# Where the sums of weights are copied and when their users wait: a two-layer Mamba-2 / attention trunk in split fp32 on one core

## The chip, the cores and the metric

One NeuronCore of a Trainium2 chip runs the whole program. The metric is the device time of one execution in microseconds. TensorE multiplies, VectorE (DVE) and ScalarE (ACT) work on tiles, GpSimd (POOL) does a few small operations and issues some DMAs, SyncE (SP) issues most DMAs.

## What is computed

The input has 256 tokens of 2048 features, in float32. Two layers work on it; each is a mixer with a residual and a SwiGLU with a residual. The first mixer is Mamba-2 (input projection, convolution, scan, gate, output projection); after layer 0 shared keys, values and forget gates are made, and the second mixer is attention with a forget bias. The part that the change touches is the SwiGLU:

```python
def swiglu(h, w_gate_up, w_down):      # h: 256 x 2048, w_gate_up: 2048 x 11264, w_down: 5632 x 2048
    g, u = jnp.split(h @ w_gate_up, 2, axis=-1)
    return (jax.nn.silu(g) * u) @ w_down
```

All weights, some 460 MB, are read from DRAM once.

## The kernel before

**Split products.** Each float32 operand is split into a rounded part `hi` and a rest `lo`; a product is three matmuls, `x_hi w_hi`, `x_hi w_lo` and `x_lo w_hi` (L562 to L564 in plain blocks, L475 to L478 in crossed groups). A load brings 128 x 1024 weights (two tiles of k by 512 columns, 512 KB) into one of six buffers `wraw`; ScalarE casts it to `whi` (L270), VectorE subtracts to get `wlo` (L276), four pieces ahead of TensorE (`SPL`).

**Blocks and pairs.** A block is 512 columns of output for all 256 tokens, in two PSUM banks `acc`. The sum over k goes in groups `kg` of 512 rows. In the output, up and down projections two neighbouring blocks make a pair (`pair`, L335): the left and the right block. In the up projection they are 512 columns of gate and the same 512 of up; 11 pairs stand in each layer. Some of the groups of a pair are "crossed": instead of eight products of (half of k) x (half of the tokens) x (block), seven products of sums do, as in Strassen's scheme (42 matmuls in place of 48). The seven are called a to g. Their products go to the two blocks' own banks (g and b to the left, f to the right) and to four more PSUM banks of the pool `mis` (d, c, a, e). The sums of activations are made on the chip (`sums_of`, L610, with a ScalarE pass over the transposes in PSUM; `add_sums`, L631, afterwards from the split halves). Of the sums of weights, in the up projection two (`c` and `a`) are made in DRAM ahead of time ("made"), and two more on VectorE between the splits (L429).

**Sums in DRAM.** A `Sum` is a DRAM tile of 512 KB: a copy of one piece of the weights, to which another is then added by an accumulating DMA. `next_sum` (L368) issues the copies of this sum and of the one after it (L377) and this sum's accumulate (L378), all in GpSimd's queue; the accumulate waits until its copy has landed. `stream` calls it before each eighth load (`PACE`, L511); were a sum still missing when its load is issued, `load` would make it there (L392). There are 84, 42 a layer.

**Order of the up projection.** With `made` and groups 1 and 2 crossed (pairs 0 to 9), a pair goes: left of group 0, right of group 0, group 1 (order "fdcaegb"), left of group 3, group 2, right of group 3. The last pair crosses group 2 alone. With the product d of a pair's first group the program issues all that is pending in the urgent and the middle list (L463), such as the transposes and splits of the blocks of `h` that the stage before has just finished. Those, too, use the banks of `mis`.

**Evictions.** With the product e, `took` (L768) starts `parts` (L732): `d` is copied out of PSUM, then VectorE makes `v = e - d`, `y = c - v`, `v = a + v`, `u = v - c`. When the left block is done, `gate` (L743) adds its two banks to `d` and `y` (which frees them for the next pair's left block) and ScalarE takes SiLU of them; when the right block is done, `up` (L751) adds its banks to `v` and `u`, multiplies, transposes and splits the result.

**Start of an up projection.** `out_stage` (L697) ends each mixer: it adds the blocks to `h`, transposes and splits them into the next stage's slots (`take`, L712), with sums of activations for the groups named in `summed` (1 and 2), sums of squares, and at the end the rsqrt of the norm on GpSimd (L581).

**Queues.** Each engine takes its instructions in the order in which the program issued them. SyncE issues the loads, each waiting until its `wraw` buffer is free. GpSimd's queue holds the copies and accumulates of the sums, the rsqrts and a few loads of the scan.

Of the kernel before, what the change touches and what calls it, by code (L numbers as in the profile page):

```python
# [9 lines left out]
F32 = mybir.dt.float32  # L10
F32R = mybir.dt.float32r
AF = mybir.ActivationFunctionType
ALU = mybir.AluOpType
# [4 lines left out]
P = 128  # L18
# [4 lines left out]
NB = 512  # L23
# [6 lines left out]
NFB = DFF // NB  # L30
# [6 lines left out]
WOUT, DN0, DN1 = (4, 6), (3, 7), (3, 6, 9)  # L37
# [1 line left out]
WARM = 9  # L39
RAW = 6  # L40
SPL = 4
PACE = 8


LAT = 0.4
# [4 lines left out]
C_AN, C_F0, C_KV, C_BN, C_F1 = 0, 16, 32, 48, 64  # L50
# [179 lines left out]
def kernel(ctx: ExitStack, tc: tile.TileContext, xT_d, x_d, cols_d, rows_d, wdt_d, win_d,  # L230
# [17 lines left out]
    def nm(s):  # L248
        uid[0] += 1
        return f"{s}_{uid[0]}"  # L250
# [114 lines left out]
            order.append(both[0].after)  # L365
        blocks.append(order + rights)

    def next_sum(n=1):  # L368

        for _ in range(n):  # L370
            i = next((i for i, v in enumerate(sums) if not v.made), None)
            if i is None:
                return
            for v in sums[i:i + 2]:
                if v.tile is None:
                    v.tile = dram.tile([P, 2, NB], F32, name=nm("wsum"))
                    nc.gpsimd.dma_start(out=v.tile, in_=v.one)  # L377
            nc.gpsimd.dma_start(out=sums[i].tile, in_=sums[i].other, accum_op=ALU.add)  # L378
            sums[i].made = True

    def slot_of(s):
        t = None
# [108 lines left out]
    def stream(pre_load, pre_split):  # L491
        pieces, units = [], []
        for b in blocks:
            for u in b.units if isinstance(b, Block) else b:
                if isinstance(u, Group):
                    pieces += [(u, n) for n in u.cross.order]
                    units += u.units.values()
                else:
                    pieces += [(u, ks) for ks in u.pieces]
                    units.append(u)  # L500
        parts = {}
        loaded, dead = [0], [0]

        def load_on():
            while dead[0] < len(units) and units[dead[0]].dead:
                dead[0] += 1
            while loaded[0] < min(dead[0] + RAW, len(units)):
                i = loaded[0]
                if i in pre_load:
                    pre_load[i]()  # L510
                if i % PACE == PACE - 1:  # L511
                    next_sum()
                load(units[i], i == 0, load_x0 if i < 2 else None)
                loaded[0] += 1

        def split_to(n):
            for i in range(len(parts), min(n, len(pieces))):
                u, js = pieces[i]
                if i in pre_split:
                    pre_split[i]()  # L520
                parts[i] = split_cross(u, js) if isinstance(u, Group) else split_piece(u, js)
                load_on()

        load_on()
        split_to(SPL - 1)
        held = deque()
        for i, (u, ks) in enumerate(pieces):
            split_to(i + SPL)
            if isinstance(u, Group):
                cross_step(u, ks, parts[i])  # L530
                continue
            b = u.blk
            nk = KT * len(b.xs)
            hi, lo, ready = parts[i]
            flow.work("E", 0.0, ready)
            if u.width < NB:
                if b.ps is None:
                    b.ps = bank([2 * u.width, T])
                for j, k in enumerate(u.ks[n] for n in ks):
                    both = hi[:, j].rearrange("p a n -> p (a n)")  # L540
                    s = slot_of(b.xs[k // KT])
                    nc.tensor.matmul(b.ps, lhsT=both, rhs=s[:, 0, k % KT, :], start=k == 0, stop=False)
                    nc.tensor.matmul(b.ps, lhsT=both, rhs=s[:, 1, k % KT, :], start=False, stop=k == nk - 1)
                flow.work("E", 0.22 * len(ks))
                if ks is u.pieces[-1]:
                    b.task = spawn(b.done(b.ps))
                continue
            if b.ps is None:
                held.append(b)
                if len(held) > 2:  # L550
                    flow.finish(held.popleft().task, evac=True)
                b.ps = [acc.tile([P, u.width], F32, tag="acc", name=nm("acc")) for _ in range(NT)]
            last = b.after is None and u is b.units[-1] and ks is u.pieces[-1]
            order = [(j, t) for j in range(len(ks)) for t in range(NT)]
            if last:
                order = [(j, t) for t in range(NT) for j in range(len(ks))]
            for n, (j, t) in enumerate(order):
                k = u.kg * KT + u.ks[ks[j]]
                s = slot_of(b.xs[k // KT])
                xh = s[:, 0, k % KT, t * P:(t + 1) * P]  # L560
                xl = s[:, 1, k % KT, t * P:(t + 1) * P]
                nc.tensor.matmul(b.ps[t], lhsT=xh, rhs=hi[:, j, :], start=u is b.units[0] and ks[j] == 0, stop=False)  # L562
                nc.tensor.matmul(b.ps[t], lhsT=xh, rhs=lo[:, j, :], start=False, stop=False)  # L563
                nc.tensor.matmul(b.ps[t], lhsT=xl, rhs=hi[:, j, :], start=False,  # L564
                                 stop=last and j == len(ks) - 1)
                if n % 2 == 1:
                    flow.work("E", STEP)
                    flow.pump()
            if last:
                finish_block(b)  # L570
        flow.finish_all()
# [4 lines left out]
    def rsqrt_of(ss, n, width):  # L576

        ms = tiny(width, "ms")
        nc.vector.tensor_scalar(out=ms, in0=ss, scalar1=1.0 / n, scalar2=EPS, op0=ALU.mult, op1=ALU.add)  # L579
        r = tiny(width, "rs")  # L580
        nc.gpsimd.tensor_tensor(out=r, in0=ms, in1=mhalf[:, :width], op=ALU.pow)  # L581
        return r
# [93 lines left out]
    def tt(out, in0, in1, op=ALU.add):  # L676
        nc.vector.tensor_tensor(out=out, in0=in0, in1=in1, op=op)  # L677
        return V(0.66)
# [15 lines left out]
            yield tt(r1, r1, w)  # L694
        return run

    def out_stage(xs, w_d, wcol, crossed, summed=()):  # L697

        ss = const.tile([P, NT, 4], F32, name=nm("ss"))
        nxt = [Slot(j in summed) for j in range(4)]  # L700
        r = [None]

        def done(j):
            def run(ps):
                for t in range(NT):
                    hb = h[:, t, j * NB:(j + 1) * NB]
                    yield tt(hb, hb, ps[t])
                yield EVAC
                nxt[j].task = spawn(take(j), flow.mid)
            return run  # L710

        def take(j):  # L712
            yield SYNC
            yield from h_slot(nxt[j], j, wcol)
            for t in range(NT):
                sumsq(h[:, t, j * NB:(j + 1) * NB], ss[:, t, j:j + 1])
                yield A(0.6)
            if j == 3:
                tot = tiny(NT, "tot")
                nc.vector.tensor_reduce(out=tot, in_=ss, axis=AX.X, op=ALU.add)  # L720
                r[0] = rsqrt_of(tot, DM, NT)

        for j in (0, 2):
            pair(xs, w_d[j:j + 2], (done(j), done(j + 1)), nxt[j:j + 2], crossed, parts_to_h(j))
        return nxt, r

    def ffn_up(xs, r, gu_d, summed):
# [4 lines left out]
        def parts(x):  # L732
            m = x.ps
            d, v, y, u = (tok(i) for i in ("d", "v", "y", "u"))
            x.part = d, y, v, u
            nc.scalar.copy(out=d, in_=m["d"])
            yield A(0.48)
            yield tt(v, m["e"], d, sub)
            yield tt(y, m["c"], v, sub)
            yield tt(v, m["a"], v)  # L740
            yield tt(u, v, m["c"], sub)

        def gate(x, ps):  # L743
            for t, g in enumerate(x.part[:2]):
                yield tt(g, ps[t], g)
            yield EVAC
            for t, g in enumerate(x.part[:2]):
                nc.scalar.activation(g, g, AF.Silu, scale=r[0][:, t:t + 1])
                yield A(0.6, SILU)
# [15 lines left out]
        for nb in range(NFB):  # L765
            x = [None]

            def took(y, x=x):  # L768
                x[0] = y
                return parts(y)  # L770

            pair(xs, gu_d[2 * nb:2 * nb + 2], (lambda ps, x=x: gate(x[0], ps), lambda ps, x=x, nb=nb: up(x[0], ps, nb)),
                 (None, acts[nb]), (1, 2) if nb < NFB - 1 else (2,), took, made=True)
        return acts


# [306 lines left out]
    for g in range(G):  # L1083
        wide(xs1, win_d[12 + g], z_done(g))

    xs2, r2 = out_stage(ys, wout_d, C_F0, WOUT, summed=(1, 2))
    act0 = ffn_up(xs2, r2, gu0_d, DN0)


# [176 lines left out]
        else:  # L1266
            wide(xsq, wv_d[j], v_done(j), wcol=C_KV)

    xs4, r4 = out_stage(oT, wo_d, C_F1, (2,), summed=(1, 2))
    act1 = ffn_up(xs4, r4, gu1_d, DN1)  # L1270
    out_v = out_d.rearrange("(t p) d -> p t d", p=P)

# [107 lines left out]
```

## Time and profile before

| | |
|---|---|
| median of 3 runs | 2597.38 us (2596.58 to 2598.68) |
| the profiled execution | 2599.11 us, span 2597.1 us |
| mean granted TensorE clock | 0.988 of full |
| busy: TensorE, weight load, VectorE, ScalarE, GpSimd | 97%, 79%, 77%, 55%, 6% |
| DMA | 591.37 MB, mean 228 GB/s |

The profile is of one execution. Times are microseconds from the start of the span unless marked ns. A group of instructions goes by line, engine and operation, written `out<-in`. Behind the bar stands the engine's idle time ahead of those instructions and what ended most of it. In a timeline the brackets hold the idle time just before an instruction and what ended it. Issue to landing is the time from the instruction that issues a DMA to its last byte. A row of busy time by stretch has the stretch, its length, then the busy time and count of instructions of PE, PEld, DVE, ACT and POOL, and last PEclk, DMA share and GB/s. PEclk is the clock that TensorE was granted, 1.00 is full speed; DMA share is the mean busy share of the 16 DMA engines (it can read a little over 1).

The stages, by the loads and matmuls of the timeline: input projection and scan to about 580 us, output projection to 714 us, up projection of layer 0 to about 1240 us, down projection to about 1500 us, attention layer to 1879 us, up projection of layer 1 to about 2360 us, down projection to the end.

### The profile page before, as it was taken

Reading aid. Unit: us, or ns where it says so; the run is one execution under the profiler, and the core shown is the slowest. Engines: PE = TensorE matmul, PEld = TensorE weight load, DVE = VectorE, ACT = ScalarE, POOL = GpSimd, SP = SyncE. Lnnn points to the kernel's source line nnn. Section 1 sums busy time; section 2 is a strip of 40 time slices with the busy share of each in tenths; the row PEclk is TensorE's granted clock in tenths of the full one; section 3 lists DMA queues with packets and bytes.
Section 4 is the critical chain, followed back from the end, with each engine's and each line's share of the span. In section 5 each row is a group of like instructions: output and inputs, shape, how many; then the busy total and the mean of one; then the engine's idle time right before and its main releaser. Section 6 shows DMA issues by size and latency. Waiting matters only on the chain.

```text
span 2597.1 us, 31677 instructions
## 1 busy us (share of the span) xinstructions
PE 2516.7 (97%) x11422; PEld 2064.6 (79%) x11422; DVE 2009.7 (77%) x2575; ACT 1437.3 (55%) x1805; POOL 153.6 (6%) x220
## 2 busy tenths in 40 slices
PE   8999999998988889999999999999989999999999
PEld 6888888887866667888888888888768888888887
DVE  6677777687876768898866766777978898988777
ACT  5666565564554445555544455665556565655544
POOL 1000000010012210000000012010000000000000
PEclk9999999999999889999999999999999999999999
DMA  8796667777579996676666677766666666665564
GB/s 287 252 297 207 187 210 219 243 225 229 201 230 331 331 330 228 217 236 206 202 209 199 196 231 227 240 203 208 212 209 220 224 225 221 228 226 173 204 241 144
DMA packets 161645, 591.37 MB, mean 228 GB/s; under 512 B 17968, under 2 KB 18624, under 8 KB 159952
## 3 DMA queue, kind: packets, MB, share of 16 engines
q1 hardware_dynamic: 135792, 490.69, 56.0%
q0 software_dynamic: 25696, 98.66, 14.5%
q8 instruction: 90, 1.47, 0.2%
q14 instruction: 67, 0.55, 0.1%
HBM read 587.10 MB, written 90.26 MB: 261 GB/s over the span
## 4 chain that ended last, share of the span: by engine, by line
PE 77%; DVE 9%; DMA 8%; ACT 3%; issue 2%; SPq 0%; ACTq 0%; DVEq 0%
PE acc L562 20%; PE acc L563 20%; PE acc L564 20%; DVE wlo L276 5%; DMA wraw<-wsum 5%; ACT whi L270 2%; DMA wraw<-in_gu_dram 2%; PE mis L475 2%; PE mis L476 2%; PE mis L478 2%; PE acc L476 2%; PE acc L478 2%; PE acc L475 2%; DVE wraw L429 2%; PE mis L594 1%
## 5 line engine op out<-in xcount | busy, mean ns | idle before, releaser
L276 DVE TENSOR_TENSOR wlo<-wraw,whi 128x1024 fp32r<-128x1024 f32 (+1 forms) x959 | 1150.1, 1220 | 370.0 <-ACT whi L270 361.0
L270 ACT CAST whi<-wraw 128x1024 fp32r<-128x1024 f32 (+1 forms) x962 | 990.6, 1049 | 757.3 <-PE acc L564 417.8
L562 PE MATMUL acc<-whi,xT 128*128 128x512 f32 x2496 | 986.7, 395 | 32.2 <-DVE d L677 25.0
L563 PE MATMUL acc<-wlo,xT 128*128 128x512 f32 x2496 | 977.3, 392 | 3.5 <-DVE wlo L276 3.3
L564 PE MATMUL acc<-whi,xT 128*128 128x512 f32 x2496 | 976.4, 391 | 0.0
L562 PEld LDWEIGHTS acc<-whi,xT 128*128 128x128 f32 x2496 | 471.1, 189 | 137.5 <-issue 34.6
L563 PEld LDWEIGHTS acc<-wlo,xT 128*128 128x128 f32 x2496 | 471.5, 189 | 103.9 <-DVE wlo L276 8.6
L564 PEld LDWEIGHTS acc<-whi,xT 128*128 128x128 f32 x2496 | 470.9, 189 | 99.0
L278 DVE SCALAR_TENSOR_TENSOR wlo<-wraw,cols,whi 128x512 fp32r<-128x512 f32 x192 | 134.7, 747 | 72.3 <-ACT whi L272 71.9
L429 DVE TENSOR_TENSOR wraw<-wraw,wraw 128x1024 f32<-128x1024 f32 x148 | 181.3, 1225 | 10.5 <-DMA wraw<-in_wout_dram 4.1
L272 ACT ACTIVATE whi<-wraw,cols 128x512 fp32r<-128x512 f32 x192 | 127.6, 717 | 72.1 <-PE acc L564 54.8
L475 PE MATMUL mis<-whi,xS 128*128 128x512 f32 x348 | 141.9, 408 | 16.8 <-ACT y L614 8.3
L476 PE MATMUL mis<-wlo,xS 128*128 128x512 f32 x348 | 142.1, 408 | 5.8 <-DVE wlo L276 5.7
L478 PE MATMUL mis<-whi,xS 128*128 128x512 f32 x348 | 140.9, 405 | 0.0
L581 POOL TENSOR_TENSOR rs<-ms,mhalf 128x4 f32<-128x4 f32 (+1 forms) x27 | 29.3, 1084 | 1223.6 <-DVE ms L579 1223.4
L476 PE MATMUL acc<-wlo,xT 128*128 128x512 f32 x224 | 88.7, 396 | 8.7 <-DVE wlo L276 8.7
L475 PEld LDWEIGHTS mis<-whi,xS 128*128 128x128 f32 x348 | 68.3, 196 | 35.9 <-ACT y L614 9.2
L378 POOL DMA_DIRECT2D wsum<-in_gu_dram x84 | 70.5, 839 | 317.5 <-DMA wsum<-in_gu_dram 317.2
L476 PEld LDWEIGHTS mis<-wlo,xS 128*128 128x128 f32 x348 | 68.4, 197 | 25.4 <-DVE wlo L276 11.3
L478 PE MATMUL acc<-whi,xT 128*128 128x512 f32 x224 | 87.8, 392 | 0.0
L475 PE MATMUL acc<-whi,xT 128*128 128x512 f32 x224 | 87.7, 392 | 0.0
L478 PEld LDWEIGHTS mis<-whi,xS 128*128 128x128 f32 x348 | 68.4, 197 | 14.2
(242 smaller groups left out, 2128.6 us busy)
## 6 DMA issues: line engine op xcount, KB each, us to landing
wraw<-in_gu_dram SPq DMA_DIRECT2D x310, 512.0 KB, 5.2
wraw<-in_dn_dram SPq DMA_DIRECT2D x176, 512.0 KB, 5.2
wsum<-in_gu_dram POOLq DMA_DIRECT2D x168, 512.0 KB, 10.3
wraw<-in_win_dram SPq DMA_DIRECT2D x159, 512.0 KB, 5.6
wraw<-wsum SPq DMA_DIRECT2D x84, 512.0 KB, 5.1
wraw<-in_wout_dram SPq DMA_DIRECT2D x64, 512.0 KB, 5.2
wraw<-in_wq_dram SPq DMA_DIRECT2D x32, 512.0 KB, 4.7
wraw<-in_wk_dram SPq DMA_DIRECT2D x32, 512.0 KB, 4.8
```

The source lines that it names most:

```text
L270: nc.scalar.copy(out=hi, in_=src)
L272: nc.scalar.activation(hi, src, AF.Copy, scale=scal)
L276: nc.vector.tensor_tensor(out=lo, in0=src, in1=hi.bitcast(F32), op=ALU.subtract)
L278: nc.vector.scalar_tensor_tensor(out=lo, in0=src, scalar=scal, in1=hi.bitcast(F32), op0=ALU.mult, op1=ALU.subtract)
L378: nc.gpsimd.dma_start(out=sums[i].tile, in_=sums[i].other, accum_op=ALU.add)
L429: nc.vector.tensor_tensor(out=us[out].raw, in0=us[in0].raw, in1=us[in1].raw, op=ALU.add)
L475: nc.tensor.matmul(ps, lhsT=xh, rhs=hi[:, p, :], start=group.first and p == 0 and name not in own, stop=False)
L476: nc.tensor.matmul(ps, lhsT=xh, rhs=lo[:, p, :], start=False, stop=False)
L478: nc.tensor.matmul(ps, lhsT=xl, rhs=hi[:, p, :], start=False, stop=stop and p == 1)
L562: nc.tensor.matmul(b.ps[t], lhsT=xh, rhs=hi[:, j, :], start=u is b.units[0] and ks[j] == 0, stop=False)
L563: nc.tensor.matmul(b.ps[t], lhsT=xh, rhs=lo[:, j, :], start=False, stop=False)
L564: nc.tensor.matmul(b.ps[t], lhsT=xl, rhs=hi[:, j, :], start=False, stop=last and j == len(ks) - 1)
```

## The change

It has three parts. The copies of the sums go to SyncE's queue, one for each call, and the accumulate that a call issues is that of the copy of the call before; a call comes before each sixth load among the first 224 and each twelfth after. In the pairs of the up projection, the last two of the four sums of products (`v = a + v`, `u = v - c`) move out of `parts` into `gate`, behind the two left evictions. The first pair of each up projection crosses group 2 alone, so that 80 sums are left; the sums of activations of group 1, first used in the second pair, are made by `add_sums` at the end of the last `take`, in the lazy list, and `took` issues what is left of them.

```diff
-PACE = 8
+PACE = (224, 6, 12)
...
-    def next_sum(n=1):
-
-        for _ in range(n):
-            i = next((i for i, v in enumerate(sums) if not v.made), None)
-            if i is None:
-                return
-            for v in sums[i:i + 2]:
-                if v.tile is None:
-                    v.tile = dram.tile([P, 2, NB], F32, name=nm("wsum"))
-                    nc.gpsimd.dma_start(out=v.tile, in_=v.one)
-            nc.gpsimd.dma_start(out=sums[i].tile, in_=sums[i].other, accum_op=ALU.add)
-            sums[i].made = True
+    def next_sum():
+        new = next((v for v in sums if v.tile is None), None)
+        old = next((v for v in sums if v.tile is not None and not v.made), None)
+        if new is not None:
+            new.tile = dram.tile([P, 2, NB], F32, name=nm("wsum"))
+            nc.sync.dma_start(out=new.tile, in_=new.one)
+        if old is not None:
+            nc.gpsimd.dma_start(out=old.tile, in_=old.other, accum_op=ALU.add)
+            old.made = True
...
-                if i % PACE == PACE - 1:
+                pace = PACE[1] if i < PACE[0] else PACE[2]
+                if i % pace == pace - 1:
                     next_sum()
...
-    def out_stage(xs, w_d, wcol, crossed, summed=()):
+    def out_stage(xs, w_d, wcol, crossed, summed=(), later=()):
...
                 r[0] = rsqrt_of(tot, DM, NT)
+                for kg in later:
+                    add_sums(nxt[kg])
...
             yield tt(v, m["e"], d, sub)
             yield tt(y, m["c"], v, sub)
+
+        def parts_of_up(x):
+            m, v, u = x.ps, *x.part[2:]
             yield tt(v, m["a"], v)
             yield tt(u, v, m["c"], sub)
...
             yield EVAC
+            yield from parts_of_up(x)
             for t, g in enumerate(x.part[:2]):
                 nc.scalar.activation(g, g, AF.Silu, scale=r[0][:, t:t + 1])
...
                 x[0] = y
+                if xs[1].adder is not None:
+                    flow.finish(xs[1].adder)
                 return parts(y)
...
-                 (None, acts[nb]), (1, 2) if nb < NFB - 1 else (2,), took, made=True)
+                 (None, acts[nb]), (1, 2) if 0 < nb < NFB - 1 else (2,), took, made=True)
...
-    xs2, r2 = out_stage(ys, wout_d, C_F0, WOUT, summed=(1, 2))
+    xs2, r2 = out_stage(ys, wout_d, C_F0, WOUT, summed=(2,), later=(1,))
...
-    xs4, r4 = out_stage(oT, wo_d, C_F1, (2,), summed=(1, 2))
+    xs4, r4 = out_stage(oT, wo_d, C_F1, (2,), summed=(2,), later=(1,))
```

## Rows read from the trace of the kernel before

**Rows 1.** Page, costliest groups: xcount | busy, mean ns | idle before, its releaser.
```profile
L276 DVE TENSOR_TENSOR wlo<-wraw,whi 128x1024 fp32r<-128x1024 f32 (+1 forms) x959 | 1150.1, 1220 | 370.0 <-ACT whi L270 361.0
...
L429 DVE TENSOR_TENSOR wraw<-wraw,wraw 128x1024 f32<-128x1024 f32 x148 | 181.3, 1225 | 10.5 <-DMA wraw<-in_wout_dram 4.1
```
**Rows 2.** Busy by stretch, up projections' pairs (last: PEclk, DMA share, GB/s).
```profile
714.20:772.06 57.86, 45.94 (x197) 36.15 (x196) 42.82 (x55) 30.63 (x45) 8.00 (x12) 0.94 0.71 219
772.06:995.75 223.69, 193.65 (x752) 146.76 (x753) 155.19 (x153) 103.08 (x110) 41.07 (x61) 0.92 1.01 322
995.75:1038.13 42.38, 41.98 (x188) 34.53 (x189) 38.17 (x39) 25.15 (x28) 0.00 (x0) 1.00 0.67 220
1879.48:1933.70 54.22, 45.41 (x198) 35.59 (x196) 42.31 (x55) 30.98 (x46) 4.31 (x6) 0.97 0.68 220
1933.70:1978.27 44.57, 42.57 (x188) 34.38 (x189) 38.44 (x39) 26.76 (x29) 0.00 (x0) 1.00 0.63 204
```
**Rows 3.** DMAs, 775 to 970 us (packets, MB, share; KB, us to landing).
```profile
q0 software_dynamic: 8808, 32.08, 61.5%
...
wsum<-in_gu_dram POOLq DMA_DIRECT2D x59, 512.0 KB, 10.9
wraw<-in_gu_dram SPq DMA_DIRECT2D x47, 512.0 KB, 16.5
```
**Rows 4.** DMAs between 995 and 1230 us.
```profile
wraw<-in_gu_dram SPq DMA_DIRECT2D x77, 512.0 KB, 4.7
```
**Rows 5.** Timeline of GpSimd, 560 to 760 us (start, duration).
```profile
592.17 0.82 POOL L378 DMA_DIRECT2D wsum<-in_gu_dram  x1 [6.74 <-DMA wsum<-in_gu_dram]
740.07 0.71 POOL L581 TENSOR_TENSOR rs<-ms,mhalf 128x2 f32<-128x2 f32 x1 [147.08 <-DVE ms L579]
```
**Rows 6.** DMAs between 100 and 350 us, input projection.
```profile
q0 software_dynamic: 3200, 13.70, 20.0%
...
wraw<-in_win_dram SPq DMA_DIRECT2D x79, 512.0 KB, 4.7
```
**Rows 7.** Timeline of SyncE's queue, 2038 to 2046 us, second group of a pair.
```profile
2039.10 1.61 SPq L398 DMA_DIRECT2D wraw<-wsum  x2
```
**Rows 8.** Timeline of ScalarE, the cast of that load.
```profile
2044.95 1.05 ACT L270 CAST whi<-wraw 128x1024 fp32r<-128x1024 f32 x1 [1.66 <-PE acc L564]
```
**Rows 9.** Timeline of TensorE at four places.
```profile
606.23 0.80 PE L476 MATMUL acc<-wlo,xT 128*128 128x512 f32 x1 [5.61 <-DVE wlo L276]
...
1899.24 0.79 PE L475 MATMUL mis<-whi,xS 128*128 128x512 f32 x1 [4.15 <-ACT y L614]
...
2050.19 0.39 PE L475 MATMUL mis<-whi,xS 128*128 128x512 f32 x1
...
2063.00 0.47 PE L562 MATMUL acc<-whi,xT 128*128 128x512 f32 x1 [0.41 <-DVE d L677]
```
**Rows 10.** Busy time by stretch, output projection of layer 0.
```profile
580.00:600.00 20.00, 18.11 (x75) 13.25 (x73) 9.70 (x9) 8.04 (x8) 3.23 (x5) 1.00 1.00 286
600.00:620.00 20.00, 14.39 (x50) 11.36 (x50) 17.14 (x17) 9.81 (x12) 0.00 (x0) 0.83 0.56 195
```
**Rows 11.** DMAs of the first 30 us.
```profile
q0 software_dynamic: 720, 2.62, 32.2%
...
wraw<-in_win_dram SPq DMA_DIRECT2D x11, 512.0 KB, 13.3
wsum<-in_gu_dram POOLq DMA_DIRECT2D x5, 512.0 KB, 10.1
```
**Rows 12.** Timeline of VectorE at the end of a pair, layer 1.
```profile
2057.57 0.69 DVE L677 TENSOR_TENSOR v<-mis,v 128x512 f32<-128x512 f32 x1
...
2060.44 0.68 DVE L677 TENSOR_TENSOR u<-v,mis 128x512 f32<-128x512 f32 x1
...
2062.18 0.68 DVE L677 TENSOR_TENSOR d<-acc,d 128x512 f32<-128x512 f32 x1
```
**Rows 13.** Waits, 1990 to 2340 us (total, times, longest).
```profile
PE acc L562 <- DVE d L677: 3.3, 8, 0.4
```

## The prediction

> **What bounds the kernel now.** The profiled execution took 2599.11 us at a span of 2597.1 us; it lies 1.7 us above the median of the runs, 2597.38 us. The sum below is made against the execution, and 1.7 us come off at the end. A difference under 0.2% (5.2 us) can't be told from no change here.
>
> The page came first: TensorE is busy for 97% of the span, so only what lets it pause, or slows it, can be had. VectorE is second, at 77%. A group of seven products asks for more of VectorE than of TensorE: seven splits and two additions of 1.22 us each [rows 1] make 11.0 us, and its 42 matmuls, at 41.98/188 = 0.223 us an instruction of a quiet pair [rows 2], make 9.4 us.
>
> The second view was busy time by stretch, one stretch for each pair of blocks of the two up projections. In the quiet state a pair takes 42.38 us, all but 0.4 of it TensorE's [rows 2]. The four pairs after the first one of layer 0 take 223.69 us together, at a granted clock of 0.92, with a DMA share of 1.01 where a quiet pair has 0.67. The two first pairs take 57.86 and 54.22 us.
>
> The third view, the DMAs of a stretch, says why: between 775 and 970 us the software queue of GpSimd holds 61.5% of the 16 engines with 59 transfers for the sums, and a weight load takes 16.5 us to land [rows 3], against 4.7 us in the quiet pairs that follow [rows 4]. The timeline of GpSimd says why there: its queue stands before the rsqrt at 740.07 us for 147 us [rows 5], and everything behind that instruction then goes out back to back. A copy on GpSimd waits for nothing but its place in that queue, so the loop's count of eight loads doesn't pace it at all.
>
> **The change, part by part.**
>
> *Copies in the load queue.* 84 copies leave GpSimd; 80 go to SyncE, each ahead of one load, and so wait with that load for a free buffer. The accumulate on GpSimd waits for a copy issued one call (6 or 12 loads) earlier, 16 us or more, so it rarely waits long, and what is behind it on GpSimd (the rsqrts, the loads of decays) waits less than now. An accumulate can still stand behind an rsqrt, but the sums are made well ahead: 36 by load 224, and by load 670, where layer 1's up projection begins, 73 of 80. None is made in haste. The burst goes, and its four pairs fall to the quiet 4 x 42.38 = 169.5 us: **-54.2 us**.
>
> What the same transfers cost elsewhere: 61.5% of 195 us over 59 transfers is 2.0 us of all 16 engines for each [rows 3], 4.0 us for a sum. In the input projection one sum in six loads (16 us) puts some 0.25 on top. Between 100 and 350 us the software queue already held 20%, and loads landed in 4.7 us [rows 6]: I take nothing there. In the up projections one sum in 12 loads is 1.5 for a pair of 18, 6 us of 42.4: 0.67 + 0.14 = 0.81, not saturated. The tightest load there is that of a sum, issued at 2039.10 us [rows 7] for a cast at 2044.95 us [rows 8], 5.9 us later, with a landing of 4.7 us. A copy right in front makes it 2.0 us longer, so the cast is 0.8 us late; the matmul that wants it starts at 2050.19 us [rows 9], 2.9 us after cast and subtraction (1.05 and 1.22 us) would be through at the usual time, and hides that. Bounds: nothing (hidden), and the burst's own price: 54.2 us over the 30 sums of its 61 GpSimd instructions [rows 2], 1.8 us a sum, for 17 sums in layer 0 and 7 in layer 1: +43 us. I take 0.25 us a sum, near the hidden end since the share is nearer the quiet one: **+6 us**.
>
> A rule bears on this. In the trace a load that shares the engines with the software queue is slowed, not stopped [rows 3]. The Trainium skill, "DMA: Bandwidth & Descriptors", section "Queues, rings and completion order", states that each engine takes turns between queues packet by packet, and goes through one ring in order. By that, a copy in the loads' own ring stands whole before the next load, where it shared before; with nothing hidden the sum would carry +48 us in place of +6 (the rival of the ring, below). No run here shows a copy in that ring yet.
>
> *The end of the first burst.* GpSimd's copies up to 592.17 us [rows 5] fall on the output projection of layer 0. There TensorE idles 20 - 18.11 = 1.9 us and then 5.61 us, and has a clock of 0.83 for 20 us [rows 9, 10]. Evenly paced, that goes: 7.5 us idle and some 2 us of slow clock, **-9.5 us** (bounds 0 and 10.9, with all 0.17 x 20 us of clock).
>
> *The start.* In the first 30 us five transfers for sums take 32.2%, 9.7 us of the engines [rows 11], in a stretch where a load takes 13.3 us to land. After the change a copy goes before load 5, another with an accumulate at load 11, two transfers fewer: **-4 us** (bounds 0 and 7.7, four fewer).
>
> *First pair with one group.* It adds six matmuls a layer, 1.3 us, and takes away three splits, two additions, two sums and a load. The new order puts 96 matmuls instead of 48 ahead of the group's second product, where all pending work on the last two blocks of the layer's input is issued. So the pauses there, 4.15 us and more [rows 9] and a clock of 0.94 and 0.97 over these pairs, are covered by 48 x 0.223 = 10.7 us of other matmuls. The sums of group 1 move behind that, as some five microseconds of VectorE work (a half of it: one addition and one subtraction over 512 columns at 0.68 us [rows 12] and four operations over 128, an estimate), due by the fifth product of the only group; the three splits and two additions that went (6.1 us) make room. The pair then takes 41.97 + 10 more instructions (198 against 188) + 6, each at 0.223, so 45.5 us: **-12.4 us** in layer 0, **-8.7 us** in layer 1 [rows 2]; the pair behind it falls from 44.57 to 42.4: **-2.2 us**. Bounds: the gain is nothing but for the burst's part (half), or a further 1.5 us each, if the transposes are counted at less than a matmul.
>
> *Up block's sums behind the left evictions.* At each pair's end VectorE does v (0.69 us) and u (0.68 us) before it takes the left banks; d ends at 2062.86 us [rows 12], and the next pair's first matmul starts at 2063.00 us, 0.41 us late [rows 9]. The same wait stands at all eight quiet boundaries of the window [rows 13]. Moved, v and u put d 1.37 us earlier, more than the wait. Next late would be the right eviction, whose banks are wanted 24 matmuls (5.4 us) later, with as much VectorE work ahead of it as now; nothing added. 20 boundaries by 0.41: **-8 us** (bounds 0 and 8.2).
>
> Sum: 54.2 + 9.5 + 4 + 12.4 + 8.7 + 2.2 + 8 - 6 = 93.0 us; 2599.1 - 93.0 - 1.7 = **2504 us**.
>
> **The rivals.**
> *Paid per sum.* The sums cost in the quiet pairs what they cost in the burst, +43 instead of +6: 2541 us. For it: the 1.2 us between the tightest load's landing and its cast. Against it: the share of 0.81, and the landings of [rows 6].
> *The ring's order.* A copy holds the loads behind it for its whole 2.0 us, 24 times in the up projections, and nothing hides it, since VectorE at 38.2 of 42.4 us [rows 2] can't catch up: 2504 - 6 + 48 = 2546 us. Against it: the 2.9 us in hand at the tightest load, and six buffers in front of the others.
> *Only the burst goes.* The first pairs stay at 54 us (their work waits elsewhere, on VectorE, which then also has the moved sums), and the boundary wait moves to the right eviction: 2504 + 8.7 + 2.2 + 6 + 8 = 2529 us.
> *Slower.* Each sum costs the burst's 1.8 us wherever it stands, in the input projection and the attention layer too: 80 x 1.8 = 144 us against 99 us of gain, 2504 - 6 + 144 = 2642 us. It decides from 99/80 = 1.24 us a sum. Against it: 20% of the engines for the software queue with loads landing in 4.7 us [rows 6].
> *It does not pace.* If accumulates still pile up behind GpSimd's rsqrts and burst, with a sum's load waiting for one, half of the 54 us stays: 2531 us. Against it: the sums are ready dozens of loads early.
>
> **How the numbers follow.** Forecast 0.60; paid per sum 0.11; the ring's order 0.07; only the burst goes 0.12; does not pace 0.05; slower 0.05. The forecast's own bounds, with first pairs 3 us shorter and the start's other 3.7 us, go to 2490; upward the first rivals reach 2546. The range is 2488 to 2546. Faster is all but the last case and a remainder: 0.94, within 0.2% 0.01, slower 0.05.
>
> **What would show it.** In the profile after: no stretch with a DMA share near 1.0 behind 35 us; loads in the up projection landing in 5 to 7 us throughout; pairs of 42.0 us in layer 0 from the second on; first pairs near 45.5 us without a pause of 4 us; no wait of the next pair's first matmul on d; no long idle before GpSimd's accumulates on the copies. The prediction is wrong if casts wait on loads right behind copies, or if the first pairs still pause.

## The result, and the profile after

The changed kernel takes 2505.9 us (2503.89 to 2506.06), the kernel before, run beside it, 2597.9 us: a ratio of 0.9645, 95% interval 0.9628 to 0.9661. The forecast was 2504 us. The profiled execution took 2506.06 us at a span of 2504.3 us.

The ledger below is read from the two traces, each stage from its first matmul to the first of the next. The list of stages above has the output projection of layer 0 begin at about 580 us; its first matmul starts at 528.6 us, and the ledger goes by that. A boundary stands for the 0.41 us that the forecast took off where one pair ends and the next begins. The differences add up to 93 us.

| stage | before, us | after, us | difference | forecast |
|---|---|---|---|---|
| start to the end of the input projection | 528.6 | 522.9 | -5.7 | -4 |
| output projection, layer 0, first pair | 99.4 | 92.3 | -7.1 | -9.5 |
| up projection, layer 0: first pair | 57.9 | 49.7 | -8.2 | -12.4 |
| its pairs 2 to 5 (the burst) | 223.7 | 166.8 | -56.9 | -54.2 and four boundaries |
| its pairs 6 to 10 | 211.9 | 208.6 | -3.3 | five boundaries |
| up projection, layer 1: first pair | 54.2 | 48.1 | -6.1 | -8.7 |
| its second pair | 44.6 | 43.4 | -1.2 | -2.2 |
| its pairs 3 to 10 | 339.0 | 333.5 | -5.4 | eight boundaries |
| all other stages | | | +1.0 | 0 |

Busy time by stretch after the change, for the pairs of [rows 2] (the same columns):

```profile
701.60:751.30 49.70, 47.01 (x203) 37.38 (x202) 41.78 (x63) 29.46 (x45) 1.91 (x2) 0.97 0.69 223
751.30:918.14 166.84, 166.84 (x753) 138.44 (x752) 151.22 (x151) 101.31 (x109) 4.91 (x6) 1.00 0.81 258
918.14:959.84 41.70, 41.70 (x189) 34.61 (x188) 38.24 (x39) 25.15 (x27) 1.63 (x2) 1.00 0.79 264
1799.21:1847.31 48.10, 45.35 (x203) 36.23 (x202) 40.81 (x62) 29.38 (x45) 2.67 (x3) 1.00 0.65 212
1847.31:1890.70 43.39, 42.29 (x189) 34.46 (x188) 37.80 (x38) 27.43 (x30) 0.81 (x1) 1.00 0.81 254
```

The four pairs of the burst now have TensorE busy for all of their 166.84 us, at full clock. The DMA share there is 0.81, the number that the prediction worked out from 0.67 and 1.5 sums a pair. GpSimd issues 6 accumulates in the stretch where it issued 61 instructions.

The DMAs between 700 and 960 us answer to [rows 3] (queue: packets, MB, share; issues: KB, us to landing):

```profile
q1 hardware_dynamic: 16696, 60.78, 68.0%
q0 software_dynamic: 1296, 4.72, 10.4%
...
wraw<-in_gu_dram SPq DMA_DIRECT2D x84, 512.0 KB, 6.1
...
wsum<-in_gu_dram SPq DMA_DIRECT2D x9, 512.0 KB, 6.5
```

A weight load takes 6.1 us to land there, not 16.5. The copies now count under SyncE's queue (q1), the accumulates under GpSimd's (q0). GpSimd's timeline, the counterpart of [rows 5]:

```profile
659.94 0.81 POOL L378 DMA_DIRECT2D wsum<-in_gu_dram  x1 [15.11 <-DMA wsum<-in_gu_dram]
679.19 0.81 POOL L378 DMA_DIRECT2D wsum<-in_gu_dram  x1 [18.43 <-DMA wsum<-in_gu_dram]
696.82 0.81 POOL L378 DMA_DIRECT2D wsum<-in_gu_dram  x1 [16.82 <-DMA wsum<-in_gu_dram]
725.38 1.08 POOL L582 TENSOR_TENSOR rs<-ms,mhalf 128x2 f32<-128x2 f32 x1 [27.74 <-DVE ms L580]
726.43 0.86 POOL L378 DMA_DIRECT2D wsum<-in_gu_dram  x1
757.64 0.81 POOL L378 DMA_DIRECT2D wsum<-in_gu_dram  x1 [30.35 <-DMA wsum<-in_gu_dram]
```

In these rows one accumulate goes every 18 to 19 us in the output projection, and one every 30 us after it. They now wait on their copies, which stand in SyncE's queue; behind the rsqrt at 725.38 us one single accumulate is due, where the whole burst ran out before.

### The profile page after: what moved, and what is told of

The parts are those of the page before. It is cut to its first block, busy times and chain, and to the rows that moved or that the text cites. A ratio compares the mean times of both kernels' runs of the same rounds, so it can differ in the third digit from the quotient of the medians.

```text
span 2504.3 us, 31677 instructions
## 1 busy us (share of the span) xinstructions
PE 2482.6 (99%) x11434; PEld 2056.0 (82%) x11434; DVE 1997.2 (80%) x2569; ACT 1425.8 (57%) x1791; POOL 105.4 (4%) x132
## 4 chain that ended last, share of the span: by engine, by line
PE 93%; DVE 3%; DMA 2%; ACT 1%; issue 1%; SPq 0%; ACTq 0%; DVEq 0%
PE acc L564 23%; PE acc L563 23%; PE acc L565 23%; PE mis L476 4%; PE mis L478 4%; PE mis L475 4%; PE acc L475 3%; PE acc L476 3%; PE acc L478 3%; DVE wlo L277 2%; PE mis L595 1%; PE mis L1032 1%; DVE wraw L429 1%; DMA wraw<-in_wout_dram 1%; ACT whi L271 1%
## 5 line engine op out<-in xcount | busy, mean ns | idle before, releaser
L476 PE MATMUL mis<-wlo,xS 128*128 128x512 f32 x336 | 131.4, 391 | 2.8 <-DVE wlo L277 2.8
L475 PE MATMUL mis<-whi,xS 128*128 128x512 f32 x336 | 130.9, 390 | 0.7 <-DVE xT L277 0.7
L478 PE MATMUL mis<-whi,xS 128*128 128x512 f32 x336 | 130.7, 389 | 0.0
L378 POOL DMA_DIRECT2D wsum<-in_gu_dram x80 | 66.5, 831 | 1406.2 <-DMA wsum<-in_gu_dram 1379.1
L476 PEld LDWEIGHTS mis<-wlo,xS 128*128 128x128 f32 x336 | 63.1, 188 | 18.1 <-DVE wlo L277 5.1
L475 PEld LDWEIGHTS mis<-whi,xS 128*128 128x128 f32 x336 | 63.0, 188 | 14.2 <-DVE xT L277 1.1
L478 PEld LDWEIGHTS mis<-whi,xS 128*128 128x128 f32 x336 | 63.1, 188 | 12.9
L271 ACT CAST xT<-mis 128x512 fp32r<-128x512 f32 x52 | 27.9, 589 | 52.4 <-PE mis L595 52.4
```

Of the source, the lines that this page charges most:

```text
L271: nc.scalar.copy(out=hi, in_=src)
L378: nc.gpsimd.dma_start(out=old.tile, in_=old.other, accum_op=ALU.add)
L475: nc.tensor.matmul(ps, lhsT=xh, rhs=hi[:, p, :], start=group.first and p == 0 and name not in own, stop=False)
L476: nc.tensor.matmul(ps, lhsT=xh, rhs=lo[:, p, :], start=False, stop=False)
L478: nc.tensor.matmul(ps, lhsT=xl, rhs=hi[:, p, :], start=False, stop=stop and p == 1)
```

## The experiments

**The queue, undone.** In the changed kernel the copies go back to GpSimd, at the same places and at the new pace.

```diff
-            nc.sync.dma_start(out=new.tile, in_=new.one)
+            nc.gpsimd.dma_start(out=new.tile, in_=new.one)
```

> The changed kernel with one word of it undone: the copies are issued by GpSimd again, at the same places of the program and at the new pace. Theory Q (the queue paces: on SyncE a copy waits with the load behind it, on GpSimd for nothing): the copies run ahead of the loads again, the burst behind the rsqrt at the end of the output projection comes back, pairs 1 to 4 of layer 0 take about 57 us each, with a DMA share near 1.0 and loads landing in over 12 us; with the pauses at the start and in the output projection about 2578 us. Rival P (the new counts of loads alone spread the sums): 2506 us, pairs of 41.7 us.

Measured: 2563.3 us, a ratio of 0.9866 (0.9851 to 0.9881) to the kernel before. Busy time by stretch of pairs 2 to 4 of layer 0 and of pair 5, then rows of the DMAs between 770 and 900 us:

```profile
765.98:928.22 162.24, 140.30 (x564) 106.89 (x565) 117.02 (x116) 78.44 (x84) 25.18 (x37) 0.94 0.96 308
928.22:969.94 41.72, 41.72 (x189) 34.61 (x188) 38.18 (x39) 25.14 (x27) 0.00 (x0) 1.00 0.68 224
```
```profile
q0 software_dynamic: 5415, 19.69, 56.9%
...
wraw<-in_gu_dram SPq DMA_DIRECT2D x31, 512.0 KB, 15.2
```

The burst is back: three pairs take 162.24 us instead of 125.1, and loads land in 15.2 us. The output projection's first pair takes 102 us, where it took 99.4 before the change and 92.3 after it. So it is the queue that paces, and the counts of 6 and 12 alone do not. The Trainium skill, "DMA: Bandwidth & Descriptors", section "Issuing engines are not separate DMA queues", says that all issuers' DMAs run on the same 16 engines, and that several issuers save only time to issue. The run agrees about the engines: in the stretch above, GpSimd's queue has 56.9% of them and SyncE's 44.3%. The 57 us between the two kernels come from when a queue lets a transfer go.

The size was missed by 15 us: the burst is shorter than in the kernel before, three pairs instead of four. That fits the sums made ahead of it: by the two traces 38 accumulates instead of 29 are out when the rsqrt comes.

**The queue alone.** The kernel before with the new `next_sum` and the new pace, and nothing else.

> The kernel before with the first part of the change alone: copies in the load queue at the new pace; first pair and evictions as before, 84 sums. Theory Q: pairs 1 to 4 of layer 0 take 42.4 us as all others do (-54 us), the output projection of layer 0 and the start gain 7 and 6 us as in the changed kernel, the first pair of layer 0 falls from 57.9 to the 54.2 us of layer 1: 2598 - 71 = 2527 us. If the sums need the other parts to be hidden: over 2535 us, with pairs above 42.4 us where sums are made.

Measured: 2523.05 us, a ratio of 0.9715 (0.97 to 0.9729). First pair of layer 0, its pairs 2 to 5, first pair of layer 1:

```profile
698.40:751.15 52.75, 46.33 (x197) 37.09 (x196) 42.47 (x55) 31.11 (x46) 2.36 (x3) 0.90 0.66 200
751.15:920.64 169.49, 167.86 (x752) 138.14 (x753) 152.73 (x153) 100.57 (x109) 4.91 (x6) 1.00 0.81 261
1804.61:1857.07 52.46, 45.26 (x197) 36.34 (x196) 42.56 (x55) 31.17 (x46) 2.37 (x3) 0.93 0.65 201
```

169.49 us are 4 x 42.37: the burst goes by this part alone, down to the quiet pair that the forecast took, and it is worth 74.5 of the 92 us. Both first pairs keep their pauses: TensorE waits 4.15 us there in layer 0 and 4.16 us in layer 1, as it did before the change. Even so they are shorter than before (57.86 and 54.22 us).

**The sums ahead of the left evictions.** The changed kernel with `v` and `u` back in `parts`.

```diff
             yield tt(y, m["c"], v, sub)
+            yield from parts_of_up(x)
...
             yield EVAC
-            yield from parts_of_up(x)
```

> The changed kernel with the up block's two sums put back ahead of the left evictions. Theory G (the left eviction is late by the two sums, and the pause costs more than its 0.41 us): each of the 20 boundaries costs 0.67 us again, pairs of 42.4 us, 2506 + 13 = 2519 us. By the prediction's own price of 0.41: 2514 us. If the pause went for another reason (fewer late loads): 2506 us.

Measured: 2518.4 us, a ratio of 0.9694 (0.968 to 0.9708), 12.5 us above the changed kernel; pairs of 42.35 to 42.44 us. TensorE's timeline at one boundary of this kernel, and the same boundary in the changed kernel:

```profile
792.25 0.39 PE L564 MATMUL acc<-wlo,xT 128*128 128x512 f32 x1
792.48 0.39 PE L565 MATMUL acc<-whi,xT 128*128 128x512 f32 x1
793.27 0.47 PE L563 MATMUL acc<-whi,xT 128*128 128x512 f32 x1 [0.41 <-DVE d L678]
793.58 0.40 PE L564 MATMUL acc<-wlo,xT 128*128 128x512 f32 x1
```
```profile
792.79 0.39 PE L565 MATMUL acc<-whi,xT 128*128 128x512 f32 x1
793.01 0.39 PE L563 MATMUL acc<-whi,xT 128*128 128x512 f32 x1
```

The reader is to see the starts, not the brackets. Matmuls start 0.227 us apart. Over the boundary the distance is 793.27 - 792.48 = 0.79 us, 0.56 too much, and the next one is 0.31, 0.08 too much: 0.65 us a boundary. The bracket says 0.41, because it counts from the end of a matmul, which the profile puts 0.39 us behind its start though the next one may start 0.227 behind it. That is the price that the forecast took too low. VectorE's timeline in the changed kernel shows the new order, `d` and `y` ahead of `v` and `u`:

```profile
790.29 0.69 DVE L678 TENSOR_TENSOR d<-acc,d 128x512 f32<-128x512 f32 x1
790.89 0.68 DVE L678 TENSOR_TENSOR y<-acc,y 128x512 f32<-128x512 f32 x1
...
792.62 0.68 DVE L678 TENSOR_TENSOR v<-mis,v 128x512 f32<-128x512 f32 x1
793.34 0.69 DVE L678 TENSOR_TENSOR u<-v,mis 128x512 f32<-128x512 f32 x1
```

`d` ends at 790.98 us, 2 us ahead of the matmul at 793.01; before, it ended 0.14 us ahead [rows 9, 12].

**The first pair with two groups.** The changed kernel with groups 1 and 2 crossed in the first pairs again and the activations' sums as before.

```diff
-                 (None, acts[nb]), (1, 2) if 0 < nb < NFB - 1 else (2,), took, made=True)
+                 (None, acts[nb]), (1, 2) if nb < NFB - 1 else (2,), took, made=True)
...
-    xs2, r2 = out_stage(ys, wout_d, C_F0, WOUT, summed=(2,), later=(1,))
+    xs2, r2 = out_stage(ys, wout_d, C_F0, WOUT, summed=(1, 2))
```

(and the same call in layer 1)

> The changed kernel with the first pair of each up projection crossing groups 1 and 2 again, the sums of activations of group 1 made as before, 84 sums. Theory F (the first pair stands because its seven products need the PSUM banks of the last transposes, whatever the DMAs do): first pairs of about 54 us in both layers in place of 49.7 and 48.1, the pause of 4 us back, 2506 + 12 = 2518 us. Rival (in layer 0 the pause came from late loads, and with even copies it is gone): first pairs of 47 us, 2503 us, since twelve matmuls are saved.

Measured: 2512.1 us, a ratio of 0.9668 (0.9652 to 0.9684). First pairs of both layers, then rows of TensorE's timeline, two in layer 0 and one in layer 1:

```profile
700.43:752.15 51.72, 45.35 (x198) 35.83 (x197) 41.26 (x53) 31.83 (x47) 2.35 (x3) 0.97 0.64 203
1800.99:1853.11 52.12, 46.23 (x197) 37.36 (x196) 42.02 (x54) 32.52 (x47) 2.36 (x3) 0.90 0.63 197
```
```profile
720.22 0.79 PE L475 MATMUL mis<-whi,xS 128*128 128x512 f32 x1 [4.16 <-ACT y L615]
...
724.89 0.47 PE L475 MATMUL mis<-whi,xS 128*128 128x512 f32 x1 [1.74 <-DVE xT L279]
...
1820.75 0.80 PE L475 MATMUL mis<-whi,xS 128*128 128x512 f32 x1 [4.15 <-ACT y L615]
```

The pause of 4.15 us stands where it stood [rows 9], in both layers, with the DMAs quiet: it is the wait of the seven products' PSUM banks for the last transposes' readers, and no late loads. The rival falls. (In layer 0 the second pause was 2.68 us before the change, so late loads had lengthened that one.) The part is worth 6.2 us, half of what was expected. The 54 us were those of the kernel before, and the queue alone had already brought these pairs to 52.75 and 52.46 us; and the new first pair has something of its own, which later runs look for.

**More sums in a pair.** Only the last number of the pace is changed, to 6 and to 4.

```diff
-PACE = (224, 6, 12)
+PACE = (224, 6, 6)
```

> The changed kernel with a sum before every sixth load throughout: 3 sums in a pair of layer 0, DMA share about 0.95. Theory H: pairs stay at 41.7 us, 2506 to 2508 us. Rival S: 5.4 us a pair, 2550 us or more. Rival of the ring (copies hold the loads behind them once they come at every sixth load): pairs of 42.5 to 45 us, 2515 to 2540 us.

> The changed kernel with a sum before every fourth load, instead of every twelfth, from load 224 on: 4.5 sums in a pair of layer 0 until all are made. Theory H (sums are free as long as the 16 engines have time left): the share reaches 1.0, pairs of 42 to 46 us in layer 0, so 2510 to 2550 us. Rival S (each sum costs the burst's 1.8 us, and the price was missed at 1.5 a pair): pairs near 50 us, 2585 us.

Measured: 2505.6 us at 6, a ratio of 0.9645 (0.9631 to 0.966); 2514.0 us at 4, a ratio of 0.9684 (0.9668 to 0.97). The four pairs from 751 us on, at 6 and at 4:

```profile
751.00:918.00 167.00, 167.00 (x755) 138.60 (x754) 151.46 (x151) 101.52 (x109) 9.66 (x12) 1.00 0.93 296
```
```profile
751.00:918.00 167.00, 165.23 (x740) 135.55 (x739) 148.73 (x148) 97.10 (x106) 13.85 (x17) 1.00 0.99 322
```

Three sums a pair, at a share of 0.93, still cost nothing. At 4.5 a pair the share is 0.99 and seven pairs take 41.9 to 43.6 us in place of 41.71, some 7 us in all of the 8 that the kernel loses. In the up projection the price is not one per sum: it begins where the engines are full. Rival S and the rival of the ring fall, as prices.

Loads do land later beside the sums. DMAs issued in the changed kernel in four microseconds from a copy on, 979.5 to 983.5 us, then in three microseconds around an accumulate, 986.5 to 989.5 us:

```profile
wraw<-in_gu_dram SPq DMA_DIRECT2D x3, 512.0 KB, 8.3
...
wsum<-in_gu_dram SPq DMA_DIRECT2D x1, 512.0 KB, 6.7
```
```profile
wraw<-in_gu_dram SPq DMA_DIRECT2D x2, 512.0 KB, 8.7
wsum<-in_gu_dram POOLq DMA_DIRECT2D x1, 512.0 KB, 9.3
```

The three loads behind this copy take 8.3 us instead of the quiet 4.7 [rows 4]. The rule of the Trainium skill that the prediction weighed ("DMA: Bandwidth & Descriptors", "Queues, rings and completion order": one ring goes in order) fits this row, but no run here shows it. What it would have made of the time, 48 us, did not come. Two loads behind the accumulate, which comes from the other queue, take 8.7 us, so sharing the engines may be the whole cause of the later landing. In the run at 6 the casts of eight pairs wait 11 times for a load to land, at most 2.2 us, and TensorE is busy through all of them. So what stands ready ahead of TensorE, the six buffers and the four pieces, covers the delay; how much each of the two covers was not tried.

**A buffer of its own for group 1's sums.** The changed kernel makes these sums in place in a free buffer, so that `took` needn't have them issued at once. (The helper that makes them in place is left out below.)

```diff
-                if xs[1].adder is not None:
-                    flow.finish(xs[1].adder)
...
-                    add_sums(nxt[kg])
+                    add_sums(nxt[kg], True)
```

> The changed kernel with a buffer of its own for the sums of activations of group 1 (made in place), so that they need not be issued at one go at the fifth product of the first pair but wherever the list of lazy work lets them, until the second pair needs them. Theory L (what is left in the first pairs, 49.7 and 48.1 us against 45.5 forecast, is that forced batch on VectorE and ScalarE): first pairs of 45 to 46 us, second pairs of 42 us, 2506 - 7 = 2499 us. Rival (VectorE is short of time there in any case): the same pauses, there or in the second pair, 2505 us.

Measured: 2510.0 us, a ratio of 0.9663 (0.9649 to 0.9678): 4 us above the changed kernel in place of 7 below, a miss. The two intervals overlap; the stages of the traces tell the kernels apart. First and second pair of layer 1, and a row of TensorE in the second:

```profile
1796.66:1842.73 46.07, 44.94 (x203) 36.15 (x202) 39.59 (x60) 28.73 (x45) 2.67 (x3) 1.00 0.73 225
1842.73:1895.68 52.95, 45.71 (x189) 36.83 (x189) 39.36 (x40) 28.10 (x30) 0.81 (x1) 0.94 0.65 204
```
```profile
1851.55 0.47 PE L564 MATMUL acc<-whi,xT 128*128 128x512 f32 x1 [3.13 <-DVE v L695]
```

The first pairs fall to 46.07 us as expected, but the second pair of layer 1 takes 52.95 in place of 43.4. There the right block waits 3.13 us for its eviction `v`, which VectorE does at 1850.72 us, behind a split that itself waits for TensorE; at 1864.65 us it waits another 3.87 us for VectorE's `u`. While the program is built it orders VectorE's pieces by its own estimate of the engines' time; that the added work made it put the split first is argued from the code and was not tried. In layer 0 the second pair loses only 1.7 us. Why the orders differ between the layers was not tried.

The same kernel without copies before load 24:

```diff
-                if i % pace == pace - 1:
+                if i >= 24 and i % pace == pace - 1:
```

> The kernel with the buffer of its own, and no copy before load 24, so that the first 30 us have no transfers for sums. Theory: TensorE's pauses of the first 13 us shrink (2.2 us of waits behind casts there), 1 to 3 us less than the kernel with the buffer alone. Rival: the first loads are late by themselves, no difference.

Measured: 2510.8 us, a ratio of 0.9668 (0.9653 to 0.9682), no difference. In the two traces the input projection ends 3.8 us earlier, and the output projection's first pair takes 93.1 instead of 90.3 us. That pair reads 89.7 to 93.1 us in the traces of the kernels with paced copies all through it, so a gain of that size ahead of it can't be told.

**Group 1's sums made early, one group in the first pair.** The changed kernel with the last arguments of the two calls put back; the lines are layer 0's, and layer 1 has the same.

```diff
-    xs2, r2 = out_stage(ys, wout_d, C_F0, WOUT, summed=(2,), later=(1,))
+    xs2, r2 = out_stage(ys, wout_d, C_F0, WOUT, summed=(1, 2))
```

> The changed kernel with one line of it undone in each layer: the sums of activations of group 1 are made early again, while the output projection's second pair runs, as in the kernel before; the first pair still crosses group 2 alone. Theory L2 (what is left in the first pairs is the late batch for group 1, and the stage before has room for it): first pairs of 45 to 46 us (49.7 and 48.1 now), second pair of layer 1 at 42 us (43.4), the output projection unchanged: 2506 - 7 = 2499 us. Rival R2 (the first pair is bound by its other work on the last two blocks): first pairs unchanged or 1 us shorter, 2504 to 2506 us, and pauses in the output projection.

Measured: 2497.0 us, a ratio of 0.961 (0.9597 to 0.9623). First pairs of both layers and second pair of layer 1:

```profile
701.09:746.19 45.10, 44.46 (x203) 36.39 (x202) 36.70 (x50) 28.93 (x44) 1.55 (x2) 1.00 0.76 245
1794.11:1839.22 45.11, 44.48 (x203) 36.39 (x202) 36.62 (x50) 28.93 (x44) 2.37 (x3) 1.00 0.73 233
1839.22:1880.92 41.70, 41.70 (x189) 34.61 (x188) 37.27 (x37) 26.41 (x29) 0.81 (x1) 1.00 0.82 252
```

45.1 us, where the forecast had 45.5, and the output projection is no longer than in the changed kernel (92.0 and 86.5 us). The late batch was all that stood between the first pairs and their forecast.

**And no sums where the loads are tight.** On top of the last kernel, no calls for sums before load 24 and between loads 160 and 200, and a sum every six loads until load 420.

```diff
-                pace = PACE[1] if i < PACE[0] else PACE[2]
-                if i % pace == pace - 1:
+                pace = 6 if i < 420 else 12
+                if (24 <= i < 160 or i >= 200) and i % pace == pace - 1:
```

> The kernel of the run before with no copies in two stretches: before load 24, and between loads 160 and 200 (the output projection's first pair, with its crossed groups); a sum before every sixth load until load 420 instead. Theory M (the 92 us of the output projection's first pair against 86.5 us of its second come from loads that share the engines with sums): that pair falls to 87 to 88 us and the start by 2 us, 2499 - 6 = 2493 us. Rival (its first pair waits for VectorE and for the work of the stage before): no difference but the start's.

Measured: 2491.0 us, a ratio of 0.9587 (0.9574 to 0.96), the best of the study, 14.9 us under the changed kernel. The output projection's first pair in the run before and in this one:

```profile
522.60:614.60 92.00, 88.53 (x397) 71.76 (x396) 76.36 (x98) 53.19 (x70) 6.57 (x8) 1.00 0.75 238
```
```profile
520.94:609.07 88.13, 87.37 (x397) 72.16 (x396) 76.59 (x98) 52.13 (x69) 2.95 (x3) 1.00 0.60 196
```

The pair is 3.9 us shorter. It reads 89.7 to 93.1 us in the other traces with paced copies, so the sums cost it 1.6 to 5.0 us, five copies, 0.3 to 1.0 us each, at a share of only 0.75. That they cost something, the medians of the two kernels show: they are 6.0 us apart, for both gaps together, while the gap at the start alone brought nothing to the kernel with the buffer of its own. Loads in that stretch land in 5.3 us instead of 7.3. TensorE is busy for 2478.1 of the 2489.7 us.

## Why the prediction was right, and where it was off

The forecast of 2504 us was met by 2505.9. Its main mechanism, the queue that paces, is shown by the run that adds it alone and by the run that undoes it alone. That the total lies within 2 us is luck. The gain was put too low by some 12 us (6 for transfers that cost nothing in the up projections, 4.5 at the boundaries, 1.7 at the start) and too high by some 10 (7.8 in the first pairs and the one behind, 2.4 in the output projection), and the two cancel. One sign that it named for being wrong did come: the first pairs still pause.

- *Copies in the load queue, -54.2 us.* Right, to the size: the queue alone makes the four pairs 169.49 us, the 169.5 of the forecast, and undoing the queue alone brings the burst back. How the transfers wait was pictured wrongly, without harm to the size. The copy does not wait for a buffer with the load behind it; it goes out as soon as the load ahead of it has been issued. One such load is issued at 979.51 us in SyncE's queue, for 0.33 us, and the copy follows 0.04 us later:

```profile
979.88 0.50 SPq L376 DMA_DIRECT2D wsum<-in_gu_dram  x1
```

  And "it rarely waits long", said of the accumulate, is wrong, as is the sign "no long idle before GpSimd's accumulates on the copies". The page of the changed kernel has 1379.1 us of such idle time:

```profile
L378 POOL DMA_DIRECT2D wsum<-in_gu_dram x80 | 66.5, 831 | 1406.2 <-DMA wsum<-in_gu_dram 1379.1
```

  GpSimd, busy for 4% of the span, has little else to do, comes to the next accumulate early, and sends it when its copy lands; "one call earlier" orders the program and not the time. It costs nothing, since TensorE does not wait for it. The count of sums ready at layer 1's up projection was off too (it begins near load 640, not 670, with 72 accumulates out, not 73); nothing hangs on that.
- *The same transfers elsewhere, +6 us.* Zero in the up projections, where pairs with 1.5 and with 3 sums read 41.7 us. The hidden end of its bounds was the true one. In the output projection's first pair, where none was priced, they cost 1.6 to 5.0 us.
- *The end of the first burst, -9.5 us.* It brought 7.1 in the profiled execution, and 9.7 in that of the queue alone, whose program is the same up to there (89.7 us). So the 2.4 us that are missing are no more than the spread of that pair, and whether they are the price of the sums that still fall on it can't be told.
- *The start, -4 us.* -5.7, within its bounds. In the first 30 us there are three transfers for sums in place of five [rows 11], as was counted: two copies, now in SyncE's queue, and one accumulate, which is all that is left of GpSimd's 32.2%:

```profile
q0 software_dynamic: 144, 0.52, 8.8%
```

- *First pair with one group, -12.4, -8.7 and -2.2 us.* -8.2, -6.1 and -1.2, and of these the queue alone brings 5.1 and 1.8 in the two first pairs; undoing the part costs 6.2 us. The step that failed is "the three splits and two additions that went (6.1 us) make room". The room is there as a sum, but the work isn't spread over it. `took` has it issued as one batch at the fifth product. Rows of VectorE's and of TensorE's timeline of the changed kernel:

```profile
736.97 0.68 DVE L641 TENSOR_TENSOR y<-xT 128x512 f32<-128x512 f32 x1
...
739.39 0.69 DVE L277 TENSOR_TENSOR xS<-xsum,xS 128x512 fp32r<-128x512 f32 x1 [0.69 <-ACT xS L271]
740.34 4.63 DVE L277 TENSOR_TENSOR wlo<-wraw,whi 128x1024 fp32r<-128x1024 f32 x4 [0.25 <-ACT whi L271]
```
```profile
740.36 0.50 PE L563 MATMUL acc<-whi,xT 128*128 128x512 f32 x1 [1.05 <-ACT whi L271]
741.62 0.50 PE L564 MATMUL acc<-wlo,xT 128*128 128x512 f32 x1 [0.76 <-DVE wlo L277]
...
743.40 0.63 PE L564 MATMUL acc<-wlo,xT 128*128 128x512 f32 x1
```

  From 736.97 to 740.08 us VectorE makes no split, and then owes four; TensorE waits, and some matmuls behind it start 0.43 us apart (743.40 to the next at 743.83), at a granted clock of 0.50, the lower of its two levels (1.2 GHz), from 743.2 to 746.0 us. With the batch made early the pairs are 45.1 us: the 45.5 stand for the order, and 4.6, 3.0 and 1.7 us were the batch's. The buffer of its own leaves the work late but lets it spread, and already brings the first pairs to 46.1 us; so most of the loss there was the issuing at one go.
- *Up block's sums behind the left evictions, -8 us.* The mechanism is right, the size was 0.67 us a boundary (42.38 to 41.71) in place of 0.41, and 12.5 us in all, by the run that undoes it, in place of 8. The upper bound, 8.2, was no bound: it took the idle time of the bracket for the time lost.
- *The parts add up:* 74.5 (queue alone) + 12.5 + 6.2 (each undone) = 93.2 us against 92.0, the first part measured by adding it, the other two by undoing them.

Of the rivals, paid per sum, the ring's order and slower fall with the pairs of 41.71 us; only the burst goes fell short of the gains that the undone parts show, though its reason, VectorE, is what held the first pairs; that it does not pace falls with GpSimd's timeline.

## What to carry to other kernels

An in-order queue is a clock: a transfer that depends on nothing runs as early as its queue lets it, whatever loop count it was written under. Put background transfers into a queue that already waits for what should pace them (here the loads, for their buffers), and keep them below a full share of the engines, with gaps where loads are tight.

Price a pause of TensorE from start to start, less the usual distance; and where work moves behind another, ask at which instruction the program issues it, not whether the engine has room over the whole stage.

## What was not expected of the hardware

Loads behind a copy between DRAM and DRAM in their own queue landed in 8.3 us in place of 4.7, and this cost nothing measurable up to a share of 0.93 in the up projections, yet 0.3 to 1.0 us a sum at a share of 0.75 in the output projection's first pair. That pair crosses a group in which VectorE makes all four sums of weights; whether that is why it has less in hand was not tried.
